# A decoder block on one core: small loads issued later, a scale block's sums cut in two, a fifth block summed on TensorE, weight loads on GpSimd's queue

## The chip, the cores and the metric

The kernel runs on one core of one Trainium2 chip (trn2). Its time is device microseconds of that core, one launch. In profiles, PE is TensorE's matmuls, PEld its weight loads, DVE is VectorE, ACT ScalarE, POOL GpSimd and SP SyncE, which only issues DMAs here.

## The reference: what is computed

One layer of a hybrid decoder block over 512 tokens of width 2048, all in float32. The part that matters here is its head:

```
mod = silu(c) @ w_ada + b_ada                     # (1, 6 * 2048); w_ada is 2048 x 12288
shift1, scale1, gate1, shift2, scale2, gate2 = split(mod, 6)
h = rms_norm(x, norm1_w) * (1 + scale1) + shift1
proj = h @ w_in                                   # 2048 x 7168: q, k, v of 8 heads, then gq, gf, gi, gg of 8 more
...
```

Behind it come the two head groups (dilated windowed attention, a gated linear recurrence), an output projection, a gated residual, and a gated MLP of width 8192 with squared ReLU. The change touches only the start, up to the second group of projections.

## The kernel before

Every product is made of three matmuls: each operand is split in a high part (float32r, made by ScalarE) and a low part (the rest, made by VectorE), and high x high, low x high and high x low are added up. A 128 x 512 matmul is the unit.

The contraction over the 2048 inputs runs over 16 blocks k of 128 rows. The gain of the norm and `1 + scale1` are both folded into the rows of `w_in`: column k of `g1c` (128 values) multiplies the weights of block k while they are split (`_split(..., scale)`, L43 and L44). So block k of the weights can't be split before column k of `g1c` exists, and that takes 2048 x 128 numbers of `w_ada` for each column. The columns come in blocks b of two (256 columns of `w_ada`, eight loads of 256 KB into `raws[b]`), one block for each pair of k. A block is summed in one of two ways:

- `summed` (blocks in `on_pe`): 16 matmuls with silu(c) as the operand, four rounds into the four row groups of a bank, then ScalarE copies, two transposes (L819), and a reduce on DVE.
- `gathered`: sixteen multiply-adds on DVE into two accumulators (L834, L836), then `to_cols`: four transposes (L159) and two row sums on ScalarE (L162).

`finish_scale` ends either (L826, L827).

`first_steps` writes out the order of PE, SP, ACT and DVE by hand (`manual_schedule`); POOL's order, and that of all engines behind it, is the scheduler's. It loads x (16 loads on SP, L845), squares it for the norm (`squares`, L785 on DVE, L788 on ACT), and takes block 0. Then it goes through the pairs k0 = 0, 2, ... 14. In pair k0, `dense(k0)` and `dense(k0 + 1)` do 18 matmuls each (six banks, three products; L883), between them lie the sums of block b = k0/2 + 1 and some transposes of x (`turn_x`, L800), and before the last third of `dense(k0 + 1)` the block is finished. At the end of the pair the weights of the next pair are split (`split_w`), which needs the columns just made. The weights of the pairs behind the first two are loaded on POOL's queue (`fetch_pair`, L767), the others and all of `w_ada` on SP.

The shift goes another way: behind the stage, background steps (`bgw`) make `shift1` from more of `w_ada` on DVE (`gemv`, L137, L139, loads L132 on SP), and then its product with some columns of `w_in`. Meanwhile `first_groups` makes the second group of projections: eight pairs again, each with two weight loads through `load_w` (L202, on SP), buffers `raw` of four. PE is given these in the scheduler's order; behind it, from the project of `gi` on, PE's order is written out.

At the very start POOL issues twelve small loads: rows of norm weights (`rows`), positions (`posi`), per-column copies of the query and key gains (`rw`, `wcol`, the latter 4 bytes a partition), two tables (`lnc_sb`, `hgm`) and the rotary frequencies (`ifq`). They are first used behind the last scale block (`mod_cols.last`), for the recurrence's bounds and the rotary tables (`rot_w`, L994 on POOL).

Of the kernel before, what the change touches and what calls it, by code (L numbers as in the profile page):

```python
# [48 lines left out]
def hybrid_block(ctx, tc, x, c, positions, norm1_w, w_ada, b_ada, w_in, q_norm_w, k_norm_w,  # L49
# [45 lines left out]
    sc_ready = dve.tensor_tensor(sc, ps_c[:, 0:NK], sc, op=ALU.mult)  # L95

    rows = ca.tile([P, P], F32, name="rows", tag="rows")
    pool.memset(rows, 0.0)
    posi = ca.tile([NT, P], I32, name="posi")
    pool.dma_start(rows[0:16], norm2_w[0].rearrange("(r p) -> r p", p=P))  # L100
    pool.dma_start(rows[16:24], attn_out_norm_w[0].rearrange("(r p) -> r p", p=P))
    pool.dma_start(rows[24:40], hg_lb_logits.rearrange("l (r p) -> (l r) p", p=P))
    pool.dma_start(rows[40:41], hg_norm_w)
    pool.dma_start(posi, positions[0].rearrange("(r p) -> r p", p=P))
    cols = const.tile([P, 48], F32, name="cols")
    n2c, aoc, hgc, posc = cols[:, 0:16], cols[:, 16:24], cols[:, 40:41], cols[:, 44:48]

    rw = ca.tile([P, 2, 32], F32, name="rw")
    wcol = ca.tile([P, 2], F32, name="wcol")
    for i, w in enumerate((q_norm_w, k_norm_w)):  # L110
        pool.dma_start(rw[:, i], w[:, 0:32].broadcast_to([P, 32]))
        pool.dma_start(wcol[:, i:i + 1], w.rearrange("o p -> p o"))
    pool.memset(wcol[0:32], 1.0)
    lnc_sb = ca.tile([P, 512], F32, name="lnc_sb")
    pool.dma_start(lnc_sb, lnc)
    hgm = ca.tile([P, NLEV, 32], F32, name="hgm")
    pool.dma_start(hgm, hgmask.rearrange("p (l t) -> p l t", t=32))
    ifq = ca.tile([P, 16], F32, name="ifq")
    pool.dma_start(ifq, inv_freq.broadcast_to([P, 16]))


    asked, marks = [None], []

# [71 lines left out]

    evacuated = []

    def load_w(view, k0, c0, n=512, eng=None, ahead=True, raws=None, behind=False, cast_behind=False, gain=None):
        with tc.high_priority() if ahead else ExitStack():
            raw = wr.tile([P, 2, n], F32, name="wraw", tag="raw", bufs=4)  # L200
            with tc.issue_after(marks[-3].ins) if behind else ExitStack():
                nc.sync.dma_start(raw, view[:, k0:k0 + 2, c0:c0 + n])  # L202
            if raws is not None:
                raws[:] = [raw[:, 0], raw[:, 1]]
            with tc.issue_after(evacuated[0].ins) if cast_behind and evacuated else ExitStack():
                return [_split(nc, wr, raw[:, j], n, eng if j else None, None if gain is None else gain[:, k0 + j:k0 + j + 1])
                        for j in range(2)]
# [38 lines left out]
    def work(name, dt=F32):  # L246
        return wk.tile([P, 512], dt, name=name, tag="wk")
# [14 lines left out]
    def first_groups(c_f, c_q, before, after):  # L262

        bt = [bank("prj", tag="mm") for _ in range(4)]
        bc = [bank("prc") for _ in range(2)]
        for k0 in range(0, NK, 2):
            before(k0)
            wt = load_w(win_v, k0, c_f, ahead=False, gain=g1c)
            wc = load_w(win_v, k0, c_q, 256, None, ahead=False, gain=g1c)
            for j in range(2):  # L270
                k = k0 + j
                ch_mm(bt, hhi[k], hlo[k], *wt[j], k == 0, k == NK - 1)
                ch_mm(bc, hhi[k], hlo[k], *wc[j], k == 0, k == NK - 1)
            after(k0)
        return bt, bc
# [439 lines left out]
    def keep(banks, name, scale=1.0):  # L715
        ts = []
        for b in banks:
            t = slot(name)
            act.activation(t, b, AF.Copy, scale=scale)
            ts.append(t)  # L720
        return ts
# [17 lines left out]
    def first_stage(c_f, c_q):  # L739

        order = mybir.EngineType
        with tc.manual_schedule(engines={order.PE, order.SP, order.Activation, order.DVE}):
            return first_steps(c_f, c_q)

    def first_steps(c_f, c_q):
# [4 lines left out]
        ssx = sm.tile([P, NT, 4], F32, name="ssx", bufs=1)  # L750
        rx = sm.tile([P, NT], F32, name="rx", bufs=1)
        raws, wraws, accs, parts = {}, {}, {}, {}
        on_pe = (0, 1, 3, 5)

        def fetch_block(b):
            raws[b] = []
# [6 lines left out]
        def fetch_pair(k0):  # L763
            wraws[k0] = []
            for c, n in ((c_f, 512), (c_q, 256)):
                raw = wr.tile([P, 2, n], F32, name="wraw", tag="raw", bufs=4)
                (pool if k0 > 2 else nc.sync).dma_start(raw, win_v[:, k0:k0 + 2, c:c + n])  # L767
                wraws[k0].append(raw)

        def split_w(k):  # L770
            parts[k] = [_split(nc, wr, raw[:, k % 2], raw.shape[2], None, g1c[:, k:k + 1]) for raw in wraws[k - k % 2]]

        def split_x(ks):
            for k in ks:
                hl = pair(k)
                hhi.append(hl[0])
                hlo.append(hl[1])
                split_to(hl, xnT[k])

        def squares(q):  # L780
            for ti in range(NT):
                jk = work("jk")
                with tc.issue_after(sc_ready.ins), tc.issue_after(sig_ready.ins):
                    if ti == NT - 1:
                        dve.tensor_tensor_reduce(jk, xs[ti][q], xs[ti][q], op0=ALU.mult, op1=ALU.add, scale=1.0, scalar=0.0,  # L785
                                                 accum_out=ssx[:, ti, q:q + 1])
                    else:
                        act.activation(jk, xs[ti][q], AF.Square, accum_out=ssx[:, ti, q:q + 1])  # L788
# [25 lines left out]
        def summed_out(b):  # L814
            t = work("acc")[:, 0:256]
            act.copy(t, accs[b][:, 0:256])
            pc = bank("pc")
            for j in range(2):
                pe.transpose(pc[:, j * P:(j + 1) * P], t[:, j * P:(j + 1) * P], ident)  # L819
            dve.tensor_reduce(g1c[:, 2 * b:2 * b + 2], pc[:, 0:256].rearrange("p (j a m) -> p j a m", j=2, m=32)[:, :, :, 0],  # L820
                              axis=AX.X, op=ALU.add)
            finish_scale(b)
# [3 lines left out]
            dve.tensor_tensor(d, d, bcol[:, NK + 2 * b:NK + 2 * b + 2], op=ALU.add)  # L826
            mod_cols.last = dve.scalar_tensor_tensor(d, d, 1.0, n1c[:, 2 * b:2 * b + 2], op0=ALU.add, op1=ALU.mult)  # L827

        def gathered(b):
            accs[b] = [work("acc")[:, 0:256] for _ in range(2)]  # L830
            for k in range(NK):
                raw, acc = raws[b][k // 2][:, k % 2], accs[b][k % 2]
                if k < 2:
                    dve.tensor_scalar(acc, raw, sc[:, k:k + 1], None, op0=ALU.mult)  # L834
                else:
                    dve.scalar_tensor_tensor(acc, raw, sc[:, k:k + 1], acc, op0=ALU.mult, op1=ALU.add)  # L836

        def gathered_out(b):
            for _ in to_cols(accs[b], g1c[:, 2 * b:2 * b + 2]):
                pass  # L840
            finish_scale(b)
# [35 lines left out]
        def dense(k, between=None):  # L877
            fine, coarse = parts.pop(k)
            first, last = k == 0, k == NK - 1
            for n, (hs, w) in enumerate(((hhi, 0), (hlo, 0), (hhi, 1))):  # L880
                for banks, ws in ((bt, fine), (bc, coarse)):
                    for j in range(len(banks)):
                        pe.matmul(banks[j], lhsT=ws[w][:, j * P:(j + 1) * P], rhs=hs[k], start=first and n == 0,  # L883
                                  stop=last and n == 2)
                if n == 1 and between:
                    between()

        def next_scale(b):
            if b in on_pe:
                summed_out(b)  # L890
            elif b < 8:
                gathered_out(b)

        for k0 in range(0, NK, 2):
            b = k0 // 2 + 1
            if k0 + 4 < NK:
                fetch_pair(k0 + 4)
            if k0 in (0, 4):
                scale_x(2 + k0 // 4, range(NT))
            if 0 < k0 < NK - 2:  # L900
                split_x((k0 + 2, k0 + 3))
            if b < 8 and b not in on_pe:
                gathered(b)
            dense(k0)
            if b in on_pe:
                summed(b, range(4))
            if k0 in (2, 6):
                turn_x(2 + k0 // 6, 0)
                turn_x(2 + k0 // 6, 1)
            dense(k0 + 1, lambda: next_scale(b))  # L910
            if k0 in (2, 6):
                turn_x(2 + k0 // 6, 2)
                turn_x(2 + k0 // 6, 3)
            if b + 2 < 8:
                fetch_block(b + 2)
            for k in (k0 + 2, k0 + 3):
                if k < NK:
                    split_w(k)
        for _ in range(16):
            bg_step()  # L920
        return bt, bc
# [9 lines left out]
    bgw.append(staggered(shift_through(4096), shift_through(3072), NK + 1, 6))  # L931
    xnT = []
    bt, bc = first_stage(4096, 3072)
    f0 = keep(bt, "f")
    hq0 = keep(bc, "gq", QS)
    with tc.issue_after(mod_cols.last.ins):
# [656 lines left out]
```

## Time and profile before

| | |
|---|---|
| median of 3 runs | 2264.39 us (2263.81 to 2265.33) |
| the profiled execution | 2263.68 us, span 2261.9 us |
| PE busy | 2215.9 us of the span |
| x landed (last piece) | 19.14 us |
| pair k0 = 0 starts on PE | 29.48 us |
| pair k0 = 14 starts on PE | 115.04 us |
| `first_groups` on PE | 123.34 to 190.14 us |
| PE's longest wait behind it | 6.17 us, up to 218.71 us |

Times in rows are microseconds from the span's start. A row of a timeline has the start, the length, the engine, the line, the operation with out<-in, the shape and a count; in square brackets stand the idle time of the engine before it and what ended it. A row of a windows view has the stretch and its length, then busy time and number of instructions of PE, PEld, DVE, ACT and POOL, the granted TensorE clock, the share of the 16 DMA engines' time that was busy, and GB/s. Matmuls are pipelined, so their ends are modelled and overlap the next start.

### The profile page before, as it was taken

To read this page: it belongs to the slowest core of one execution; us is meant where nothing else is said; L and a number is where in the kernel's file an instruction comes from. 1 tells how busy PE (TensorE), PEld (TensorE's weight loads), DVE (VectorE), ACT (ScalarE), POOL (GpSimd) and SP (SyncE) were. 2 spreads that over 40 slices of the span, in tenths; PEclk is the share of its full clock that TensorE was granted. 3 is DMA by queue.
4 is the path that set the end of the run, shared out by engine and by line. 5 is a ranking of instruction groups with operands and counts; after the bars stand their busy time and mean duration, and the time that the engine had idled before them with its cause. 6 is when DMAs were issued, how large, how long until landed. Compare 5 with 4: busy or idle time off the path is not lost.

```text
span 2261.9 us, 33188 instructions
## 1 busy us (share of the span) xinstructions
PE 2215.9 (98%) x11889; PEld 1825.1 (81%) x11889; DVE 1788.2 (79%) x2707; ACT 1093.6 (48%) x1923; POOL 449.9 (20%) x677
## 2 busy tenths in 40 slices
PE   5898999999999999999999999999999999999999
PEld 4687888888888888888887888888888888888887
DVE  4699888678886557778648988998897779967878
ACT  5356344443354464457544565565554333443332
POOL 2100022000220000003232323332232222222221
PEclk9999999999999999999999999999999999999999
DMA  9779564556555248847879789889979987998884
GB/s 327 242 257 336 177 197 163 182 180 210 184 164 187 74 142 279 275 123 261 325 276 358 288 308 390 304 301 360 337 288 368 369 315 258 348 346 312 302 298 166
DMA packets 260660, 598.30 MB, mean 265 GB/s; under 512 B 23220, under 2 KB 42432, under 8 KB 260496
## 3 DMA queue, kind: packets, MB, share of 16 engines
q1 hardware_dynamic: 183360, 327.75, 42.8%
q0 software_dynamic: 72064, 258.93, 31.2%
q10 hardware_dynamic: 5072, 9.51, 1.3%
q8 instruction: 93, 1.52, 0.3%
q14 instruction: 71, 0.58, 0.1%
HBM read 518.49 MB, written 77.61 MB: 264 GB/s over the span
## 4 chain that ended last, share of the span: by engine, by line
PE 82%; DMA 6%; DVE 5%; issue 5%; POOL 1%; ACT 1%; SPq 0%; ACTq 0%; POOLq 0%; DVEq 0%
PE f L1351 13%; PE f L1349 13%; PE f L1350 13%; PE prj L213 8%; PE prj L215 8%; PE prj L214 8%; PE f L223 3%; PE f L221 2%; PE f L222 2%; PE prj L223 1%; PE prj L222 1%; PE prj L221 1%; DMA araw<-in_w_ada_dram 1%; DMA Fl<-f_lod 1%; PE pho L643 1%
## 5 line engine op out<-in xcount | busy, mean ns | idle before, releaser
L1333 ACT CAST vhi<-raw 128x1024 fp32r<-128x1024 f32 x392 | 413.4, 1055 | 518.7 <-PE f L1351 409.5
L1334 DVE TENSOR_TENSOR vlo<-raw,vhi 128x1024 fp32r<-128x1024 f32 x392 | 474.7, 1219 | 139.4 <-ACT vhi L1333 139.1
L1350 PE MATMUL f<-vlo,Fh 128*128 128x512 f32 x1376 | 535.8, 389 | 0.5 <-DVE vlo L1334 0.4
L1351 PE MATMUL f<-vhi,Fl 128*128 128x512 f32 x1376 | 535.6, 389 | 0.4 <-DMA Fl<-f_lod 0.4
L1349 PE MATMUL f<-vhi,Fh 128*128 128x512 f32 x1376 | 536.0, 390 | 0.0
L40 ACT CAST whi<-wraw 128x512 fp32r<-128x512 f32 x304 | 187.1, 621 | 363.1 <-PE prj L215 277.8
L213 PE MATMUL prj<-whi,hi 128*128 128x512 f32 x896 | 360.4, 402 | 0.6 <-ACT aq L361 0.5
L215 PE MATMUL prj<-whi,lo 128*128 128x512 f32 x896 | 350.5, 391 | 0.2 <-DVE lo L255 0.2
L214 PE MATMUL prj<-wlo,hi 128*128 128x512 f32 x896 | 349.7, 390 | 0.0
L41 DVE TENSOR_TENSOR wlo<-wraw,whi 128x512 fp32r<-128x512 f32 x304 | 209.2, 692 | 156.4 <-ACT whi L40 151.3
L1350 PEld LDWEIGHTS f<-vlo,Fh 128*128 128x128 f32 x1376 | 258.3, 188 | 55.4 <-DVE vlo L1334 2.0
L1351 PEld LDWEIGHTS f<-vhi,Fl 128*128 128x128 f32 x1376 | 258.3, 188 | 54.6 <-DMA Fl<-f_lod 0.9
L1349 PEld LDWEIGHTS f<-vhi,Fh 128*128 128x128 f32 x1376 | 258.3, 188 | 53.4
L1317 DVE TENSOR_TENSOR raw<-raw,raw 128x1024 f32<-128x1024 f32 x224 | 269.8, 1217 | 4.3 <-DMA raw<-in_w_ff_dram 3.9
L139 DVE SCALAR_TENSOR_TENSOR acc<-araw,sc,acc 128x512 f32<-128x512 f32 x280 | 201.8, 748 | 21.0 <-DMA araw<-in_w_ada_dram 20.3
L215 PEld LDWEIGHTS prj<-whi,lo 128*128 128x128 f32 x896 | 168.6, 188 | 36.9 <-DVE lo L255 0.6
L213 PEld LDWEIGHTS prj<-whi,hi 128*128 128x128 f32 x896 | 168.8, 188 | 35.3 <-ACT ak L361 0.9
L214 PEld LDWEIGHTS prj<-wlo,hi 128*128 128x128 f32 x896 | 169.0, 189 | 32.8
L1295 POOL DMA_DIRECT2D Fh<-f_hid x112 | 79.2, 707 | 427.2 <-PE f L1351 412.1
L223 PE MATMUL f<-hi,wlo 128*128 128x512 f32 x256 | 99.9, 390 | 0.9 <-DVE wlo L41 0.9
L221 PE MATMUL f<-hi,whi 128*128 128x512 f32 x256 | 100.3, 392 | 0.0
L222 PE MATMUL f<-lo,whi 128*128 128x512 f32 x256 | 99.6, 389 | 0.0
(338 smaller groups left out, 2978.8 us busy)
## 6 DMA issues: line engine op xcount, KB each, us to landing
raw<-in_w_ff_dram SPq DMA_DIRECT2D x224, 512.0 KB, 10.3
araw<-in_w_ada_dram SPq DMA_DIRECT2D x384, 256.0 KB, 4.2
Fh<-f_hid POOLq DMA_DIRECT2D x112, 512.0 KB, 6.4
Fl<-f_lod POOLq DMA_DIRECT2D x112, 512.0 KB, 7.5
wraw<-in_w_in_dram SPq DMA_DIRECT2D x98, 512.0 KB, 4.8
Fh<-h_hid POOLq DMA_DIRECT2D x60, 512.0 KB, 6.6
Fl<-h_lod POOLq DMA_DIRECT2D x60, 512.0 KB, 7.6
f_hid<-part POOLq DMA_DIRECT2D x48, 512.0 KB, 7.4
```

The source lines that it names most:

```text
L41: _split.low = (eng or nc.vector).tensor_tensor(lo, src, hi.bitcast(F32), op=ALU.subtract)
L139: dve.scalar_tensor_tensor(acc, raw[:, k - k0], vec[:, k:k + 1], acc, op0=ALU.mult, op1=ALU.add)
L213: pe.matmul(banks[ti], lhsT=hi[:, ts], rhs=whi, start=first, stop=False)
L214: pe.matmul(banks[ti], lhsT=hi[:, ts], rhs=wlo, start=False, stop=False)
L215: pe.matmul(banks[ti], lhsT=lo[:, ts], rhs=whi, start=False, stop=last)
L223: pe.matmul(banks[j], lhsT=wlo[:, js], rhs=hi, start=False, stop=last)
L1317: dve.tensor_tensor(dst, a, b, op=ALU.subtract)
L1333: cast_done.append(act.copy(hi, src))
L1334: split_done.append(dve.tensor_tensor(lo, src, hi.bitcast(F32), op=ALU.subtract))
L1349: pe.matmul(banks[t], lhsT=fh[u][a][:, ts], rhs=whi[:, a], start=first, stop=False)
L1350: pe.matmul(banks[t], lhsT=fh[u][a][:, ts], rhs=wlo[:, a], start=False, stop=False)
L1351: pe.matmul(banks[t], lhsT=fl[u][a][:, ts], rhs=whi[:, a], start=False, stop=end)
```

## The change

- The twelve small loads and the two memsets that go with them are issued behind `fetch_pair(12)` (its second load is marked, and they wait for its issue), in place of before everything else.
- In `squares`, DVE takes two of each four pieces of x in place of one.
- `gathered` takes a range of k: the first eight k of block b + 1 stand between `split_w` of the next pair's two k, the other eight at the head of the next pair, ahead of `split_x`. Before, all sixteen stood behind `split_x`.
- Block 7 joins `on_pe`.
- `split_x` stands ahead of `scale_x`.
- In `first_groups`, the weights go on POOL's queue in place of SP's.

```diff
-    pool.memset(rows, 0.0)
-    pool.dma_start(rows[0:16], norm2_w[0].rearrange("(r p) -> r p", p=P))
...
-    pool.dma_start(ifq, inv_freq.broadcast_to([P, 16]))
...
-    def load_w(view, k0, c0, n=512, eng=None, ahead=True, raws=None, behind=False, cast_behind=False, gain=None):
+    def load_w(view, k0, c0, n=512, eng=None, ahead=True, raws=None, behind=False, cast_behind=False, gain=None, queue=nc.sync):
...
-                nc.sync.dma_start(raw, view[:, k0:k0 + 2, c0:c0 + n])
+                queue.dma_start(raw, view[:, k0:k0 + 2, c0:c0 + n])
...
-            wt = load_w(win_v, k0, c_f, ahead=False, gain=g1c)
-            wc = load_w(win_v, k0, c_q, 256, None, ahead=False, gain=g1c)
+            wt = load_w(win_v, k0, c_f, ahead=False, gain=g1c, queue=pool)
+            wc = load_w(win_v, k0, c_q, 256, None, ahead=False, gain=g1c, queue=pool)
...
-        on_pe = (0, 1, 3, 5)
+        on_pe = (0, 1, 3, 5, 7)
...
-                (pool if k0 > 2 else nc.sync).dma_start(raw, win_v[:, k0:k0 + 2, c:c + n])
+                d = (pool if k0 > 2 else nc.sync).dma_start(raw, win_v[:, k0:k0 + 2, c:c + n])
+                if k0 == NK - 4:
+                    marks[:] = [d]
...
-                    if ti == NT - 1:
+                    if ti % 2:
...
-        def gathered(b):
-            accs[b] = [work("acc")[:, 0:256] for _ in range(2)]
-            for k in range(NK):
+        def gathered(b, ks):
+            if b not in accs:
+                accs[b] = [work("acc")[:, 0:256] for _ in range(2)]
+            for k in ks:
...
+            if b < 8 and b not in on_pe:
+                gathered(b, range(8, NK))
+            if 0 < k0 < NK - 2:
+                split_x((k0 + 2, k0 + 3))
             if k0 in (0, 4):
                 scale_x(2 + k0 // 4, range(NT))
-            if 0 < k0 < NK - 2:
-                split_x((k0 + 2, k0 + 3))
-            if b < 8 and b not in on_pe:
-                gathered(b)
             dense(k0)
...
-            for k in (k0 + 2, k0 + 3):
-                if k < NK:
-                    split_w(k)
+            if k0 + 2 < NK:
+                split_w(k0 + 2)
+                if b + 1 < 8 and b + 1 not in on_pe:
+                    gathered(b + 1, range(8))
+                split_w(k0 + 3)
...
     bt, bc = first_stage(4096, 3072)
+    with tc.issue_after(marks.pop().ins):
+        pool.memset(rows, 0.0)
+        pool.dma_start(rows[0:16], norm2_w[0].rearrange("(r p) -> r p", p=P))
...
+        pool.dma_start(ifq, inv_freq.broadcast_to([P, 16]))
```

More of the change, by code (lines that the diff above doesn't have):

```diff
@@ L97, in hybrid_block @@
     rows = ca.tile([P, P], F32, name="rows", tag="rows")
-    pool.memset(rows, 0.0)
     posi = ca.tile([NT, P], I32, name="posi")
-    pool.dma_start(rows[0:16], norm2_w[0].rearrange("(r p) -> r p", p=P))
[L101 to L104, printed above, removed]
     cols = const.tile([P, 48], F32, name="cols")
@@ L109, in hybrid_block @@
     wcol = ca.tile([P, 2], F32, name="wcol")
[L110 to L113, printed above, removed]
     lnc_sb = ca.tile([P, 512], F32, name="lnc_sb")
-    pool.dma_start(lnc_sb, lnc)
     hgm = ca.tile([P, NLEV, 32], F32, name="hgm")
-    pool.dma_start(hgm, hgmask.rearrange("p (l t) -> p l t", t=32))
     ifq = ca.tile([P, 16], F32, name="ifq")
-    pool.dma_start(ifq, inv_freq.broadcast_to([P, 16]))
     asked, marks = [None], []
@@ L886, in dense @@
                     between()
[L888 to L892, printed above, removed]
         for k0 in range(0, NK, 2):
@@ L897, in first_steps @@
                 fetch_pair(k0 + 4)
+            if b < 8 and b not in on_pe:
+                gathered(b, range(8, NK))
+            if 0 < k0 < NK - 2:
+                split_x((k0 + 2, k0 + 3))
             if k0 in (0, 4):
                 scale_x(2 + k0 // 4, range(NT))
-            if 0 < k0 < NK - 2:
-                split_x((k0 + 2, k0 + 3))
-            if b < 8 and b not in on_pe:
-                gathered(b)
             dense(k0)
-            if b in on_pe:
+            if b < 8 and b in on_pe:
                 summed(b, range(4))
@@ L909, in first_steps @@
                 turn_x(2 + k0 // 6, 1)
-            dense(k0 + 1, lambda: next_scale(b))
+            dense(k0 + 1, lambda: None if b > 7 else (summed_out if b in on_pe else gathered_out)(b))
             if k0 in (2, 6):
@@ L933, in hybrid_block @@
     bt, bc = first_stage(4096, 3072)
+    with tc.issue_after(marks.pop().ins):
+        pool.memset(rows, 0.0)
+        pool.dma_start(rows[0:16], norm2_w[0].rearrange("(r p) -> r p", p=P))
+        pool.dma_start(rows[16:24], attn_out_norm_w[0].rearrange("(r p) -> r p", p=P))
+        pool.dma_start(rows[24:40], hg_lb_logits.rearrange("l (r p) -> (l r) p", p=P))
+        pool.dma_start(rows[40:41], hg_norm_w)
+        pool.dma_start(posi, positions[0].rearrange("(r p) -> r p", p=P))
+        for i, w in enumerate((q_norm_w, k_norm_w)):
+            pool.dma_start(rw[:, i], w[:, 0:32].broadcast_to([P, 32]))
+            pool.dma_start(wcol[:, i:i + 1], w.rearrange("o p -> p o"))
+        pool.memset(wcol[0:32], 1.0)
+        pool.dma_start(lnc_sb, lnc)
+        pool.dma_start(hgm, hgmask.rearrange("p (l t) -> p l t", t=32))
+        pool.dma_start(ifq, inv_freq.broadcast_to([P, 16]))
     f0 = keep(bt, "f")
```

## The prediction

> **What bounds the kernel now.** I read the page's busy shares and its chain first, then the windows by stage, then the chain and timelines of the first 220 us.
>
> ```profile
> PE 2215.9 (98%) x11889; PEld 1825.1 (81%) x11889; DVE 1788.2 (79%) x2707; ACT 1093.6 (48%) x1923; POOL 449.9 (20%) x677
> PE 82%; DMA 6%; DVE 5%; issue 5%; POOL 1%; ACT 1%; SPq 0%; ACTq 0%; POOLq 0%; DVEq 0%
> 0.00:20.00 20.00, 0.45 (x1) 0.18 (x1) 3.39 (x13) 9.59 (x27) 9.00 (x24) 1.00 0.88 283
> 20.00:120.00 100.00, 89.42 (x492) 65.76 (x493) 63.42 (x159) 45.79 (x94) 9.78 (x13) 0.98 0.85 271
> 120.00:200.00 80.00, 80.00 (x360) 66.17 (x359) 75.62 (x148) 47.97 (x98) 4.41 (x9) 1.00 0.88 301
> 200.00:220.00 20.00, 13.83 (x63) 11.30 (x62) 20.00 (x35) 11.88 (x25) 0.15 (x1) 0.90 1.03 376
> 220.00:2262.00 2042.00, 2032.16 (x10978) 1681.73 (x10976) 1625.75 (x2355) 978.34 (x1681) 426.58 (x631) 1.00 0.74 261
> ```
>
> The window rows give the busy time of PE, PEld, DVE, ACT and POOL, then clock, DMA share and GB/s. PE idles 46.0 us of the 2261.9 us span: 19.6 before 20 us, 10.6 between 20 and 120, none between 120 and 200, 6.2 between 200 and 220, and 9.8 in the 2042 us behind. Everything the change touches lies before 220 us. Behind that PE never stops for long, so a lead that PE has at 220 us should reach the end whole; the question is what lead it gets.
>
> **Part 1: the start.** The first 19 us load x.
>
> ```profile
> 13.64 5.50 DMA xs<-in_x_dram
> 4.00:12.00 8.00, 0.45 (x1) 0.18 (x1) 1.21 (x6) 3.24 (x11) 4.04 (x11) 1.00 0.90 256
> 12.00:18.00 6.00, 0.00 (x0) 0.00 (x0) 1.40 (x4) 3.55 (x11) 1.93 (x4) 1.00 1.05 385
> lnc_sb<-in_lnc_dram POOLq DMA_DIRECT2D x1, 256.0 KB, 7.7
> hgm<-in_hgmask_dram POOLq DMA_DIRECT2D x1, 96.0 KB, 7.7
> L785 DVE CUSTOM_DVE_ANT_0 jk<-xs x4: 682/692/693, 8.7 to 19.3; 128x512 f32<-128x512 f32 x4
> L788 ACT ACTIVATE jk<-xs x12: 617/626/630, 8.5 to 18.6; 128x512 f32<-128x512 f32 x12
> ```
>
> The chain goes from the last piece of x (issued 13.64, landed 19.14) to its square and on. From 4 to 12 us, with the small loads on POOL's queue, the DMA engines moved 256 GB/s at a share of 0.90; from 12 to 18 it was 385. The change takes the small loads out of there. Full rate over those 8 us would be 1.03 MB or 2.7 us more, and the two tables (lnc, hgm: 0.36 MB) leave another 0.9 us of room: 3.6 us at most. Part of the slow rate may be the queue's own start, so I take 3.0. The lower bound is the bytes alone, 0.9. Negative I exclude: nothing is added before x. The scale blocks and weights follow x on the same queue, so they and PE's start move with it.
>
> Squares: ACT had 12 and DVE 4, now 8 each. The last piece is squared by DVE before and after (0.69 us). ACT's twelve, at 0.62 from 8.5 us, could have ended at 16, so this edit is worth nothing at an x that lands at 16.1, and keeps ACT from being the bound if x lands sooner. DVE's four more (2.8 us) lie in its waits for x. I count 0.
>
> **Part 2: the pairs of k (20 to 123 us).** Each pair costs PE 36 matmuls; the scale columns for the next pair must exist before PE can start it.
>
> ```profile
> 41.17 1.19 PE L883 MATMUL prj<-hi,whi 128*128 128x512 f32 x4
> 50.38 0.85 PE L159 MATMUL pc<-ident,acc 128*128 128x128 f32 x4 [1.21 <-DVE acc L836]
> 54.84 1.20 PE L883 MATMUL prj<-hi,whi 128*128 128x512 f32 x4 [1.34 <-ACT whi L43]
> 65.70 1.19 PE L883 MATMUL prj<-hi,whi 128*128 128x512 f32 x4
> 79.36 1.20 PE L883 MATMUL prj<-hi,whi 128*128 128x512 f32 x4 [1.35 <-ACT whi L43]
> 90.23 1.19 PE L883 MATMUL prj<-hi,whi 128*128 128x512 f32 x4
> 92.33 1.29 DVE L255 TENSOR_TENSOR lo<-xnT,hi 128x512 fp32r<-128x512 f32 x2
> 94.06 5.62 DVE L836 SCALAR_TENSOR_TENSOR acc<-araw,sc,acc 128x256 f32<-128x256 f32 x14
> 99.44 0.92 PE L159 MATMUL pc<-ident,acc 128*128 128x128 f32 x4 [2.11 <-DVE acc L836]
> 100.05 2.02 PE L883 MATMUL prj<-hi,wlo 128*128 128x512 f32 x4
> 101.47 0.16 DVE L826 TENSOR_TENSOR g1c<-g1c,bcol 128x2 f32<-128x2 f32 x1 [1.78 <-ACT pc L162]
> 102.72 1.50 PE L883 MATMUL prj<-hi,whi 128*128 128x512 f32 x4
> 111.85 0.30 PE L159 MATMUL pc<-ident,acc 128*128 128x128 f32 x1 [1.71 <-DVE acc L836]
> 115.04 1.20 PE L883 MATMUL prj<-hi,whi 128*128 128x512 f32 x4 [0.41 <-ACT whi L43]
> 100.00:110.00 10.00, 10.00 (x39) 7.71 (x37) 7.71 (x19) 4.12 (x10) 0.00 (x0) 0.83 0.49 140
> ```
>
> The starts of pairs 2, 4, 6, 8, 10, 12 and 14 are 41.17, 54.84, 65.70, 79.36, 90.23, 102.72 and 115.04. Pairs 4 and 8, whose block (3, 5) is summed on TensorE, take 10.86 and 10.87. Pairs 2, 6, 10 and 12, whose block (2, 4, 6, 7) DVE sums, take 13.67, 13.66, 12.49 and 12.32, and in each PE waits for DVE's last acc. In DVE's order the two lows of x (lo, 1.29) stand ahead of all sixteen accs.
>
> - Halves round the low part: the sixteen accs stay the same work, but lo moves behind them, into the 1.78 us in which DVE waits for ACT's row sums anyway. DVE's last acc comes 1.29 sooner. Pairs 2 and 6 can use what PE waits there, 1.2 each; their second wait (1.34, on ACT behind the copies of xnT) moves along but stays. Pair 10 gains 1.3. The price: the second k's low weights come half the accs later (3.1 us), 5.3 us behind the pair's start, and PE reads them as the last third of the second k, 6.8 us or more behind it. Cover 1.5; if it went, the gain of 1.3 would go with it. So the bounds are 0 and 1.3 a pair.
> - The wait of 2.11 in pair 10 is followed by matmuls at half speed (2.02 for four that take 1.07 to 1.2 elsewhere; granted clock 0.83 in that window). Most of it is hidden behind ACT; 1.50 against 1.20 in the next pair's first four is what shows: 0.3.
> - Fifth block on TensorE: pair 12 becomes a pair like 4 and 8: 12.32 to 10.87, 1.45. DVE loses 6 us of accs there and idles, since its order is written out. ScalarE copies one row more, as in pairs 4 and 8.
> - ACT's scale_x and split_x change places: both are done inside the same pair. Nothing.
>
> Sum of part 2: 1.2 + 1.2 + 1.3 + 0.3 + 1.45 = 5.4 (bounds 1.4 to 5.6: block 7 alone, or all of it).
>
> The Trainium skill ("TensorE: Matmul & The Clock Gate", Part 1) has the clock halve after an idle window of about 3.4 us. Here 2.11 was enough, and 1.71 in pair 12 was not; by that page alone pair 10 would owe its 0.3 to something else, and the sum would be 5.1.
>
> **Part 3: the small loads in their new place.** They are issued behind pair 12's weights (81.46 to 82.90).
>
> ```profile
> 92.32 1.45 POOL L767 DMA_DIRECT2D wraw<-in_w_in_dram  x2 [9.42 <-DVE wlo L44]
> 80.00:92.00 12.00, 11.93 (x77) 8.65 (x76) 5.03 (x13) 4.68 (x10) 1.44 (x2) 1.00 0.73 225
> ```
>
> POOL stands idle 9.42 us there and the DMA engines run at 0.73. Twelve issues at not over 0.73 (the row's two weight loads took 1.45) and two memsets, one of them behind a landing (7.7 for the tables above), are 8.8 + 7.7: they may push pair 14's loads back some 7 us. Those are first read for pair 14 (115.04): cover 15 us or more, cost 0. The small tiles are first used behind the last block's columns, near 114: cover 20 us, cost 0.
>
> **Part 4: weights on POOL's queue (123 to 190 us).**
>
> ```profile
> 123.34 0.39 PE L221 MATMUL prc<-hi,whi 128*128 128x512 f32 x1
> 190.14 0.39 PE L213 MATMUL prj<-whi,hi 128*128 128x512 f32 x1
> wraw<-in_w_in_dram SPq DMA_DIRECT2D x20, 512.0 KB, 6.1
> wraw<-in_w_in_dram POOLq DMA_DIRECT2D x6, 512.0 KB, 5.2
> 121.65 3.34 SPq L202 DMA_DIRECT2D wraw<-in_w_in_dram  x2
> 133.86 7.41 SPq L202 DMA_DIRECT2D wraw<-in_w_in_dram  x3
> 142.50 1.56 POOL L994 TENSOR_TENSOR rot_w<-sinT,rw 128x64 f32<-128x64 f32 x4 [48.73 <-DVE sinT L988]
> 169.78 0.49 DVE L137 TENSOR_SCALAR acc<-araw,sc 128x512 f32<-128x512 f32 x1 [1.00 <-DMA araw<-in_w_ada_dram]
> 218.71 1.11 PE L159 MATMUL pc<-ident,acc 128*128 128x128 f32 x4 [6.17 <-DVE acc L153]
> ```
>
> Sixteen weight loads leave SP, where they wait for a free buffer (7.41 us for three) with the scale tiles queued behind them. On POOL they cost 0.73 of issue each (above) and nothing is queued behind them but rot_w and each other; they land no later there (5.2 against 6.1). PE does not wait in this stretch, so the loads themselves bring it nothing. What can gain is DVE, which is full from 120 on and ends late: PE stands 6.17 at 212 to 218.7 for it. Scale tiles that come sooner take away DVE's one wait for them, 1.00. I take 1.0; bounds 0 and, if DVE's order fell so that its backlog vanished, 6.2. The eight pairs of this stage take PE from 123.34 to 190.14, 8.35 each; with two pairs of buffers a load may come some 8 us late before PE sees it.
>
> The Trainium skill ("DMA: Bandwidth & Descriptors", Issuing engines are not separate DMA queues) says that all issuing queues share the same DMA engines and a second one saves only issue time. By that page part 4 is worth 0 and the sum is 8.4; the 7.41 us that SP stood is more than issue time.
>
> **Sum.** 3.0 + 5.4 + 1.0 = 9.4 us. The profiled execution took 2263.68, of which 1.8 lies outside its span; 2263.7 - 9.4 = 2254.3. It was 0.7 faster than the median of the runs (2264.39), so I predict 2255.0.
>
> **Rivals.**
>
> - x lands hardly sooner, since the slow rate up to 12 us is the queue's start: 0.9 instead of 3.0, 2257.1. For it: 0.90 share, the engines were not idle. Against: the rate recovers just as POOL's loads end.
> - The lead is lost at 212 us: DVE (20.00 of 20.00) or the scale tiles behind it (DMA share 1.03) end when they did, and PE only waits longer at the same transposition, 6.2 + 8.4. Then 2264, no change. For it: both are full there. Against: DVE's part of that work starts right behind the last pair's low weights, which come sooner too, and its accs of block 7 are gone.
> - The backlog vanishes: 5.2 us more than forecast, 2249.8.
> - Slower: rot_w stands in POOL's stream ahead of a weight load. If the third pair's loads (121.65) had to stand behind rot_w (142.50 to 146.5), they would be 25 us late; landing (5.2) and split would have it ready at 153, PE takes that pair at 123.34 + 16.7 = 140.0, so PE loses 13 less the 9.4 gained: 2268.0. From about 22 us late (9 of cover here, 9.4 of gain, 4 of margin) it decides the sign. For it: rot_w waits long on DVE. Against: another place in the stream avoids it.
>
> **How the numbers follow.** Forecast 0.62; x hardly sooner 0.13; lead lost 0.12; backlog gone 0.07; POOL blocked 0.06. A run cannot tell less than 0.2% (4.5 us) from no change. Faster: the first two and the fourth, 0.82, less 0.02 for sums of small misses; same 0.13; slower 0.07. Range 2248 to 2260: the bounds of the parts add up to 2.3 and 15.4 us of gain, of which it takes in 4 to 16, and it leaves out the lost lead and the blocked queue, 0.18.
>
> **What the next profile would show.** Part 1: the window 4 to 12 us above 320 GB/s, x landed near 16. Part 2: pairs 2, 6 and 10 shorter by 1.2 to 1.6, pair 12 near 10.9, no half clock near 95. Part 4: no wait on scale tiles near 160, PE's wait before its late transposition not over 6.2. Wrong if that wait has grown by the lead, if POOL stands before weights, or if DVE, which asks for a block's first tiles some 2 us sooner, then waits for them.

## The result, and the profile after

After: 2260.31 us, median of 20 runs (2257.27 to 2266.36); before, 20 runs on the same chip: 2264.78 (2262.44 to 2266.01, and one of 5783.21). The ratio is 0.9982, interval 0.9975 to 0.9989: 4.1 us gained (4.5 between the medians). The forecast was 2255.0, a gain of 9.4, in a range of 2248 to 2260. The profiled execution of after took 2260.87 us.

The windows of after (columns as before), with the page's busy line ahead of them:

```profile
PE 2218.3 (98%) x11919; PEld 1825.0 (81%) x11919; DVE 1784.7 (79%) x2700; ACT 1090.2 (48%) x1912; POOL 461.0 (20%) x693
```

```profile
4.00:12.00 8.00, 0.45 (x1) 0.18 (x1) 3.11 (x12) 3.14 (x10) 0.00 (x0) 1.00 0.98 325
12.00:18.00 6.00, 0.58 (x4) 0.22 (x4) 3.14 (x10) 2.38 (x8) 0.01 (x1) 1.00 1.04 345
...
20.00:120.00 100.00, 94.58 (x545) 70.82 (x542) 63.76 (x160) 48.71 (x99) 19.74 (x32) 1.00 0.88 285
120.00:200.00 80.00, 79.62 (x357) 65.22 (x356) 74.75 (x140) 47.78 (x102) 11.81 (x19) 1.00 0.89 309
200.00:220.00 20.00, 13.45 (x54) 10.80 (x53) 19.15 (x33) 13.30 (x26) 0.00 (x0) 0.83 0.89 327
220.00:2259.00 2039.00, 2027.64 (x10953) 1677.19 (x10951) 1619.76 (x2345) 972.50 (x1667) 426.21 (x631) 1.00 0.74 261
```

Between 4 and 12 us the DMA engines moved 325 GB/s where they moved 256. Behind 220 us PE idles 11.4 us (2039.00 less 2027.64) where it idled 9.8. The last piece of x, from the chain, and PE's timeline of the pairs and of every wait that matters behind them:

```profile
10.78 5.75 DMA xs<-in_x_dram
```

```profile
38.19 1.20 PE L871 MATMUL prj<-hi,whi 128*128 128x512 f32 x4
50.66 1.20 PE L871 MATMUL prj<-hi,whi 128*128 128x512 f32 x4 [1.34 <-ACT whi L43]
61.52 1.20 PE L871 MATMUL prj<-hi,whi 128*128 128x512 f32 x4
73.97 1.20 PE L871 MATMUL prj<-hi,whi 128*128 128x512 f32 x4 [1.34 <-ACT whi L43]
84.84 1.19 PE L871 MATMUL prj<-hi,whi 128*128 128x512 f32 x4
92.84 0.85 PE L144 MATMUL pc<-ident,acc 128*128 128x128 f32 x4 [0.91 <-DVE acc L824]
95.97 1.19 PE L871 MATMUL prj<-hi,whi 128*128 128x512 f32 x4 [0.89 <-ACT whi L43]
106.96 1.20 PE L871 MATMUL prj<-hi,whi 128*128 128x512 f32 x4
115.25 0.39 PE L206 MATMUL prc<-hi,whi 128*128 128x512 f32 x1
175.74 1.21 PE L208 MATMUL prj<-hi,wlo 128*128 128x512 f32 x4 [0.38 <-DVE wlo L44]
211.93 1.11 PE L144 MATMUL pc<-ident,acc 128*128 128x128 f32 x4 [6.55 <-DVE acc L138]
1019.90 0.50 PE L208 MATMUL f<-hi,wlo 128*128 128x512 f32 x1 [1.24 <-DVE wlo L41]
1222.84 0.50 PE L1348 MATMUL f<-vlo,hi 128*128 128x512 f32 x1 [0.45 <-DVE vlo L1332]
1228.12 0.44 PE L1377 MATMUL pt<-ident,s 128*128 128x128 f32 x2 [2.01 <-DVE s L1396]
1710.80 0.50 PE L1349 MATMUL f<-vhi,Fl 128*128 128x512 f32 x1 [0.76 <-DMA Fl<-f_lod]
```

x landed at 16.53 (19.14 before). The rows at L871 are the starts of pairs 2, 4, 6, 8, 10, 12 and 14. So pairs 2, 6, 10 and 12 took 12.47, 12.45, 11.13 and 10.99, each 1.2 to 1.4 less than before, and the first group starts at 115.25, 8.09 us sooner. The forecast had 8.4 for parts 1 and 2. Then PE gives the lead back: matched against the same matmuls of before, it leads by 8.1 at 124 us, 7.1 at 225, 6.3 at 1030, 3.1 at 1240 and 2.8 at the end (places by the times of before; at 225 the half clock behind the wait near 212 is over in both). Where PE stood 6.55, 1.24, 2.01 and 0.76 from 211.93 on, it had stood 6.17, 0.64, 1.56 and 0.43 before.

### The profile page after: what moved, and what is told of

Same layout as the page of the kernel before. It is cut to its first block, busy times and chain, and to the rows that moved or that the text cites. A ratio compares the mean times of both kernels' runs of the same rounds, so it can differ in the third digit from the quotient of the medians.

```text
span 2259.1 us, 33229 instructions
## 1 busy us (share of the span) xinstructions
PE 2218.3 (98%) x11919; PEld 1825.0 (81%) x11919; DVE 1784.7 (79%) x2700; ACT 1090.2 (48%) x1912; POOL 461.0 (20%) x693
## 4 chain that ended last, share of the span: by engine, by line
PE 71%; issue 9%; DMA 9%; DVE 7%; POOL 3%; ACT 1%; SPq 0%; POOLq 0%; ACTq 0%; DVEq 0%
PE f L1349 10%; PE f L1348 10%; PE f L1347 10%; PE prj L198 8%; PE prj L200 7%; PE prj L199 7%; PE f L208 2%; PE f L207 2%; PE f L206 2%; DMA Fl<-h_lod 2%; PE prj L871 1%; DMA f_lod<-fs 1%; PE prj L206 1%; PE prj L208 1%; PE prj L207 1%
## 6 DMA issues: line engine op xcount, KB each, us to landing
raw<-in_w_ff_dram SPq DMA_DIRECT2D x224, 512.0 KB, 10.6
```

## The experiments

The late loss was the question. Each version was run against the kernel before on its own chip; ratios are to that.

| version | us (runs) | ratio to before, interval |
|---|---|---|
| start only | 2261.82 (11) | 0.9986, 0.9977 to 0.9995 |
| POOL's queue only | 2265.25 (11) | 1.0003, 0.9994 to 1.0012 |
| pairs only | 2264.21 (11) | 0.9995, 0.9987 to 1.0004 |
| after, weights back on SP | 2260.63 (11) | 0.9985, 0.9976 to 0.9994 |
| after, small loads at the start | 2263.24 (11) | 0.9993, 0.9985 to 1.0002 |
| after + 8 sums in pair 12 | 2255.66 (5) | 0.9961, 0.9949 to 0.9974 |
| after + 48 small matmuls | 2255.87 (5) | 0.9961, 0.9947 to 0.9974 |
| after + 96 | 2260.59 (11) | 0.9982, 0.9973 to 0.9991 |
| after + 128 | 2263.64 (11) | 0.9989, 0.9980 to 0.9998 |
| before + 16 | 2266.81 (11) | 1.0008, 0.9999 to 1.0017 |
| before + 32 | 2270.50 (11) | 1.0021, 1.0012 to 1.0030 |
| 8 sums in pair 12 + 48 | 2252.75 (5) | 0.9944, 0.9931 to 0.9956 |
| 8 sums in pair 12 + 96 | 2255.01 (5) | 0.9956, 0.9943 to 0.9968 |
| 6 sums in pair 12 + 48 | 2253.45 (5) | 0.9945, 0.9932 to 0.9957 |

**The parts alone, and second profiles of both kernels.** The start alone has the small loads behind pair 12's weights and the new squares; POOL's queue alone has `queue=pool` in `first_groups`.

> The changed kernel once more, for a second profile. In the first one PE leads the kernel before by 8.1 us at pair 14, 7.2 near 990 us and 2.8 at the end; behind 225 us the instruction streams of both kernels are the same. Theory A (the late loss is chance: how the loads of two queues interleave while the DMA engines are full, and where a wait of PE falls in the clock's window): the lead up to 900 us comes out within 0.3 of the first profile, and what is lost behind 990 us differs by over 1 us or falls on other waits. Theory B (a kernel that leads runs into the same full DMA queue, so the lead is cut at fixed places): the same waits, within 0.5 us each (1.24 near 1020, 0.45 near 1223, 2.0 near 1228 and 0.76 near 1711), and half clock at 1229 again.

> The kernel before once more, for a second profile. Theory A: its late waits (0.64 near 1026, 1.56 near 1233, 0.43 near 1714) change too, by up to 1 us, and a wait above 1.7 may bring half clock. Theory B: they stay within 0.2 us.

> The kernel before with the small loads moved behind pair 12's weights and the squares two and two, nothing else. The prediction has 3.0 us for it. Expected: the first pair of k starts at 26.5 in place of 29.5. If a lead reaches the end whole, 2261.8 (3.0 under the kernel before). If the late stage eats leads (theory B), 1 us under it or less.

> The kernel before with only the sixteen weight loads of the second group on GpSimd's queue. The prediction has a gain of 1.0 for it, the rival 0. The trace of the changed kernel rather shows a lead that falls by 0.9 between 130 and 190 us: by that, 0 to 1 us slower than the kernel before, with the wait near 212 us longer than 6.2.

The start is worth 3.2 us, as forecast (3.0), and its lead stays: 3.7 at 225 us, 4.1 at 1240, 3.8 at the end. POOL's queue is worth nothing. A chance lead of 0.5 up to pair 12 was -0.2 at 124 us, ahead of the loads that were moved: half clock had followed the wait of 2.10 in pair 12. From 124 to 219 it fell to -1.04. DVE waited 1.68 for the scale tiles near 170 (1.00 before), and PE 6.52 for DVE (6.17):

```profile
111.24 0.30 PE L159 MATMUL pc<-ident,acc 128*128 128x128 f32 x1 [2.10 <-DVE acc L836]
```

```profile
170.64 0.49 DVE L137 TENSOR_SCALAR acc<-araw,sc 128x512 f32<-128x512 f32 x1 [1.68 <-DMA araw<-in_w_ada_dram]
```

```profile
219.75 1.12 PE L159 MATMUL pc<-ident,acc 128*128 128x128 f32 x4 [6.52 <-DVE acc L153]
```

The second profile of after had the same 2.01 near 1226, and that execution took 2257.4. So the wait belongs to the kernel; the stretch of half clock that followed it in the first profile (a window of it is below) does not. The second profile of before (2265.88) had its late waits within 0.8 us of the first one's, with one more of 1.24 at 1714.

**Pairs only, and after with one part taken back.**

> The kernel before with the pairs' edits alone: halves round the low part, the order of the splits, block 7 on TensorE. Small loads stay at the start, squares as before, weights on SP. Prediction's theory (the lead that the pairs give reaches the end whole): pair 0 near 29.5, pairs 2, 6, 10 and 12 at 12.5, 12.5, 11.1 and 11.0, PE's first group behind the pairs 5.1 to 5.4 us sooner than before, and the time 5.1 to 5.4 us below before, near 2259.7. Rival (the pairs' lead is largely lost behind 123 us: -3.2 for the start and +0.7 for POOL's queue leave only -1.6 of the -4.1 for the pairs): the same pairs and the same lead at 123, but 1 to 2.5 us below before, with PE's waits near 175, 212, 1019 and 1228 together 3 us longer than in before.

```diff
-        on_pe = (0, 1, 3, 5)
+        on_pe = (0, 1, 3, 5, 7)
...
+            if b < 8 and b not in on_pe:
+                gathered(b, range(8, NK))
```

> The kernel after with the sixteen weight loads of the first groups back on SP's queue. Prediction's theory (POOL's queue is worth 1.0): 1 us slower than after, 2261.3. Rival (POOL's queue loses the lead it should keep, as it did alone: 1.6 us between 115 and 219): 0.7 to 1.5 us faster than after, 2259 to 2259.6; no PE wait near 175, and PE's lead over before at 219 us 0.8 to 1.6 above after's 7.2. If neither: the same as after, and the losses lie elsewhere.

> The kernel after with the small loads back at the start. If the parts add up: the start's 3.0 go, 2263.2 to 2263.5, pair 0 near 29.5. If late places take back a part of any lead: less than that is lost, 1 to 2 us (2261.5 to 2262.5), with PE's waits near 1019 and 1228 smaller than after's 0.9 to 1.2 and 2.0.

Pairs only: PE's lead grew from 0.7 at pair 0 to 5.8 at 124 us, 5.1 from the pairs, and was 1.9 at the end. The rival held: of the 5.4 that the pairs were to bring, 1.1 us came out (0.0005 of 2264), and the interval allows for no gain at all. The wait at 212, 7.23 long, took 1.2 of the lead, the stretch near 1230 with its wait of 2.00 took 1.5. With the small loads back at the start, after loses 2.9 between the medians: that part adds up. Taking POOL's queue back changed nothing that can be told (0.9985 against 0.9982), with the wait near 212 longer by as much as PE came sooner:

```profile
211.82 1.12 PE L144 MATMUL pc<-ident,acc 128*128 128x128 f32 x4 [7.64 <-DVE acc L138]
```

**The wait near 212.** Since block 7 went to TensorE, DVE stands 6.06 us in pair 12 of after:

```profile
105.42 0.17 DVE L807 TENSOR_REDUCE g1c<-pc 128x2 f32<-128x8 f32 x1 [6.06 <-PE pc L806]
```

Eight of the sixteen background steps (`gemv`'s sums) were moved there:

```diff
+            if k0 == NK - 4:
+                for _ in range(8):
+                    bg_step()
...
-        for _ in range(16):
+        for _ in range(8):
```

> The kernel after, with eight of the sixteen background sums (0.74 each) that DVE does at the first group moved into pair 12, where DVE stands idle some 6 us since block 7 went to TensorE. If the wait near 212 is DVE's amount of work and a lead at 220 reaches the end: PE's wait falls from 6.5 to 1 to 2, the lead over before at 220 rises from 7.2 to about 12, and the time falls by 3 to 5 to 2255.5 to 2257.5. If a kernel with a lead loses it to the full DMA queues further on (waits near 1019, 1228, 1711): the wait at 212 is gone all the same, but those three grow by as much, and the time stays 2259 to 2260. If the scale tiles' landings set that wait (DMA share 1.03 there): it stays near 6.5.

The wait at 212 is gone, and a smaller one stands at 184:

```profile
184.03 0.80 PE L198 MATMUL prj<-whi,hi 128*128 128x512 f32 x1 [2.67 <-ACT f L704]
```

The lead at 225 us was 12.9, and 3.1 of it went behind that (after: 4.3 of 7.1, in its second profile 1.7 of 8.0; weights on SP: 2.0 of 7.0; pairs only: 2.7 of 4.6; loads first: 1.6 of 3.7; start only: none of 3.8). The loss does not grow with the lead, so that theory falls. Near 1230 every one of these versions with block 7 on TensorE loses 0.6 to 3.3 us, and none without it does.

**What block 7 moves.** PE's own instructions come by DMA, on queue 8. The list of queues, before and after:

```profile
q8 instruction: 93, 1.52, 0.3%
```

```profile
q8 instruction: 94, 1.54, 0.3%
```

Each is one packet of 16 KB, and takes one of the 16 DMA engines about 1 us. One comes every 28.4 us where PE is full, and in that time PE does some 125 matmuls and 125 weight loads (133 and 132 in the 30 us below): one load is 256 instructions or nearly so. Block 7 on TensorE adds 32 sums and spares two transposes: 30 matmuls (11919 against 11889) with their weight loads, 60 instructions, nearly a quarter of a load. So all later loads should come 6 to 7 us forward, by that estimate. Near 1195 to 1225 the DMA engines are full:

```profile
1195.00:1225.00 30.00, 29.92 (x133) 24.44 (x132) 23.22 (x23) 13.44 (x15) 7.08 (x10) 1.00 1.03 383
```

There a piece of weights (`raw`) lands late or not, DVE starts on it at once and works in a fixed order, and 11 us later PE stands for DVE's `s`. In before, POOL issues the Fh load at 1204.07 (POOL's timeline), one instruction load falls between 1217.8 and 1219.8 (the queues in that window), and the piece lands for DVE at 1221.71 (DVE's timeline), 17.6 behind POOL's issue; PE waits 1.56:

```profile
1204.07 0.71 POOL L1295 DMA_DIRECT2D Fh<-h_hid  x1 [4.41 <-PE f L1351]
```

```profile
q8 instruction: 1, 0.02, 3.4%
```

```profile
1221.71 1.23 DVE L1317 TENSOR_TENSOR raw<-raw,raw 128x1024 f32<-128x1024 f32 x1 [1.72 <-DMA raw<-in_w_ff_dram]
```

```profile
1232.87 0.44 PE L1379 MATMUL pt<-ident,s 128*128 128x128 f32 x2 [1.56 <-DVE s L1398]
```

In after the issue is at 1197.72, the instruction load between 1205 and 1207, while all the pieces are still on their way, and the piece lands at 1216.96, 19.2 behind the issue:

```profile
1197.72 0.70 POOL L1293 DMA_DIRECT2D Fh<-h_hid  x1 [3.23 <-PE f L1349]
```

```profile
q8 instruction: 1, 0.02, 3.5%
```

```profile
1216.96 1.22 DVE L1315 TENSOR_TENSOR raw<-raw,raw 128x1024 f32<-128x1024 f32 x1 [2.16 <-DMA raw<-in_w_ff_dram]
```

To test it, the loads were moved and nothing else: small matmuls that nothing reads, on the same line of the code, in PE's idle time at the start.

```diff
-    sc_ready = dve.tensor_tensor(sc, ps_c[:, 0:NK], sc, op=ALU.mult)
+    sc_ready = dve.tensor_tensor(sc, ps_c[:, 0:NK], sc, op=ALU.mult); [pe.matmul(ps_c[0:32, P:P + 8], lhsT=ident[:, 0:32], rhs=crow[:, 0:8], start=True, stop=True) for _ in range(96)]
```

> The kernel after with 96 small matmuls (32x8) in PE's idle time at the start (7.9 to 17.4 us); nothing reads them. PE's instructions are loaded 16 KB at a time through one of the DMA engines, about 1 us each and one every 28.4 us; block 7's 32 more transpositions brought that load 7 us forward, in all six runs with the pairs' edit into the full DMA stretch near 1195 to 1225. 96 matmuls with their weight loads are 192 instructions, three quarters of a load: the loads return to where the kernel before has them. Theory (where PE's instruction load falls sets the loss there): counted from the Fh issue at 1197.7, the load at +14.3 in place of +7.9, the weights issued at +2.2 land at 17.0 to 17.6 in place of 18.7 to 19.2, PE's wait at the transpositions near 1228 falls from 2.0 to 0.8 to 1.5, the one near 1711 from 0.8 to 0.4, and the time is 1 to 2.5 us below after's (2258 to 2259.3). Rival (the lead itself runs into the full queues, whatever PE loads): load and landing part, the wait stays 2.0, the time 2260.3.

> The control: the kernel after with 128 such matmuls at the start, 256 instructions, one whole load, so that the later loads fall where after has them. Theory: load at +7.9, landing at 18.7 to 19.2, PE's wait 2.0 and the time as after (2260 to 2261). If the small matmuls help or harm by themselves (a warm clock, a later start), it shows here as in the version with 96.

> The kernel before with 32 such matmuls at the start, 64 instructions, as many as block 7 on TensorE adds, and nothing else. Theory: PE's instruction load moves from +14.3 to +7.9 after the Fh issue near 1204.1, the weights issued at +2.2 land at 18.2 to 19.3 in place of 16.8 to 17.6, PE's wait near 1231 grows from 0.8 to 1.6 toward 2.0 (it is capped there by DVE's own order), the one near 1712 from 0.4 to 0.8, and the time is 0.5 to 1.5 us above before. Rival: no change in landing or time.

> Eight background sums in pair 12 (2255.7 alone) and the 96 small matmuls together. Theory: the two gains add up, 2253.5 to 2255; PE's lead over before keeps 11 of the 12.9 us that it has at 223. Rival: 2255.7, with the wait of 2.0 near 1217 still there.

The count was wrong: PE's timeline shows each small matmul twice.

```profile
7.56 10.36 PE L95 MATMUL ps_c<-crow,ident 128*32 128x8 f32 x191 [0.94 <-DVE sc L95]
```

So 32 and 96 moved the loads by half a load, not by a quarter and three quarters, into the full stretch again (4.3 us ahead of POOL's issue in after + 96, 1.6 behind it in before + 32), and the landings stayed late, or became so: 18.7 and 19.2. Before + 32 took 5.8 us more than before. In its profile 2.9 of that go near 1029, at a wait of 1.95 with half clock behind it (granted clock 0.57 in the window), and 1.4 near 1239, at a wait of 2.01; that the first of these too is due to a load is not shown.

```profile
1029.16 0.50 PE L223 MATMUL f<-hi,wlo 128*128 128x512 f32 x1 [1.95 <-DVE wlo L41]
```

```profile
1029.00:1033.00 4.00, 3.84 (x10) 3.02 (x11) 4.00 (x8) 4.00 (x8) 2.01 (x4) 0.57 0.80 257
```

The control with 128 (two whole loads) had loads, landing and wait as in after, and queue 8 brought two packets more than in after, which fits 256 instructions to a load; its small matmuls end near 21.5 and start pair 0 4.0 us later, enough for the 3.3 us between the medians. The next set had the counts that were wanted:

> The kernel after with 48 of the small matmuls at the start. In the versions with 32 and 96 each of them showed as two matmuls with two weight loads, so that 32 moved PE's instruction loads by half a load, 96 by one and a half, and 128 by two. 48 are 192 instructions, three quarters of a load: what was wanted. Theory (where PE's instruction load falls): counted from the Fh issue near 1197.7, loads at -13 to -14.5 and +14 to +15 and none between; the weights issued at +2.2 land at 16.8 to 17.6, PE's wait near 1228 is 0.8 to 1.6, and the time 1 to 2.5 us below after's, 2258 to 2259.5. Rival: loads there, but landing and wait as in after, 2260.4.

> The kernel before with 16 of the small matmuls at the start, 64 instructions, as many as block 7 on TensorE adds. Theory: loads at about -21 and +7.5 after the Fh issue near 1204; landing of the weights issued at +2.2 at 18.2 to 19.3 in place of 16.8 to 17.6, PE's wait near 1231 1.8 to 2.0, and the time 0.7 to 2 us above before's. Rival: 2264.5 as before, with its wait.

> Eight background sums in pair 12 and 48 of the small matmuls: 2255.7 without them. Theory: PE's instruction load leaves the full stretch, 2253.5 to 2255, landing at 16.8 to 17.6 after the Fh issue and a wait below 1.7 near 1217. Rival: 2255.0 to 2255.7, wait 2.0.

> Six background sums in pair 12 in place of eight, with 48 of the small matmuls. With eight, PE waits 2.7 near 184 for DVE's low weights and not at all at 212; with none, 6.5 at 212. If DVE's work up to 212 is one sum that is only shared out between these two waits: the wait at 184 falls to about 1, one of 1 to 2 us comes back at 212, and the time is within 1 us of the version with eight. If the wait at 184 is DVE's order there (eight is too many at that place): 1 to 2 us faster.

After + 48: loads at -10.9 and +14.9; POOL's issue at 1197.98, the piece lands at 1214.17, and PE waits 0.59:

```profile
1197.98 0.71 POOL L1293 DMA_DIRECT2D Fh<-h_hid  x1 [3.25 <-PE f L1349]
```

```profile
1214.17 1.23 DVE L1315 TENSOR_TENSOR raw<-raw,raw 128x1024 f32<-128x1024 f32 x1 [0.61 <-DMA raw<-in_w_ff_dram]
```

```profile
211.47 1.12 PE L144 MATMUL pc<-ident,acc 128*128 128x128 f32 x4 [6.55 <-DVE acc L138]
...
1225.79 0.44 PE L1377 MATMUL pt<-ident,s 128*128 128x128 f32 x2 [0.59 <-DVE s L1396]
```

Its wait at 212 is that of after, 6.55, and its lead over before is 6.7 at 225 us, 7.0 at 1240 and 6.7 at the end. It takes 2255.87, 4.4 us less than after, by work that nothing reads. The 4.4 lies between a median of 20 runs and one of five, and the two intervals just part (0.9975 and 0.9974). Before + 16 is the reverse: the load moves to +7.5, the landing from 17.6 to 19.3, PE's waits to 1.89 (1028) and 2.00:

```profile
1225.52 1.23 DVE L1317 TENSOR_TENSOR raw<-raw,raw 128x1024 f32<-128x1024 f32 x1 [2.00 <-DMA raw<-in_w_ff_dram]
```

```profile
1236.68 0.44 PE L1379 MATMUL pt<-ident,s 128*128 128x128 f32 x2 [2.00 <-DVE s L1398]
```

Its 2266.81 is 1.9 above before; the interval just reaches 1. Six sums in pair 12 spoke against the theory, and were profiled a second time, as was after + 48:

> A second look at the version with 48 small matmuls. If the place of PE's instruction loads sets the landing: loads at -11 and +15 again, the weights issued at +2.2 land at 16 to 17.6, PE's wait near 1226 is below 1.6. If the first look was chance: landing 18 to 19 and a wait of 2.0.

> A second look at the one profile that spoke against it: loads at -10.5 and +14.9, and yet landing at 18.6 and a wait of 2.0. If that was chance (two queues' packets fall in another order): landing 16 to 17.6 this time. If this kernel has another reason: 18.6 again.

The two executions took 2257.25 and 2254.96. So the second profile of after + 48 is only 0.15 faster than that of after: it was 1.1 us behind it at 225 us, by a later start, and gained 2.1 in the stretch near 1228, where neither had half clock.

All profiles of the stretch, counted from POOL's Fh issue (instruction loads of 16 KB from 15 us ahead of it to 25 behind; landing of the piece issued 2.2 us behind it, 3.1 in before + 32; PE's wait for `s`):

| | loads | landing | PE's wait |
|---|---|---|---|
| before, two profiles; start only; POOL only | -14.7 to -13.9 and +14.2 to +14.4 | 16.8 to 17.6 | 0.79 to 1.56 |
| after + 48, two profiles; 8 sums + 48 | -11.0 to -10.3 and +14.8 to +14.9 | 16.0 to 16.5 | 0.59 |
| 6 sums + 48, two profiles | -10.9, -10.6 and +14.8 | 17.8, 18.6 | 1.74, 2.00 |
| after + 96; 8 sums + 96 | -4.7, -4.3 and over +24 | 17.8, 18.7 | 1.75, 2.01 |
| before + 32 | +1.6 | 19.2 | 2.01 |
| before + 16; after, two profiles; after + 128; weights on SP; loads first; pairs only; 8 sums | +7.5 to +8.0 | 18.2 to 19.5 | 2.00 to 2.01 |

With no load between -10 and +14 the piece lands by 17.6 in seven of nine profiles; with one there, in none of eleven. The gap is narrow: the earliest of the late ones is 17.8. The first piece of the group, issued some 0.5 us behind POOL's load, shows the same: 8.8 to 9.1 in the first two rows, 9.3 to 10.3 in all others. That is later by about the 1.1 us that a load takes; how one packet on one DMA engine delays a piece was not followed. The exception is one kernel, late in both profiles from the first piece on, with its loads where after + 48 and 8 sums + 48 have theirs. Why it is late stays open, so the place of the load explains 18 of 20 profiles and not all. The 8 KB loads of the other engines (queue 14) are not the cause: after and after + 48 both have them at -0.5 to +0.1 and +9.2.

**The version that beats both.** Eight sums in pair 12 with 48 small matmuls: 2252.75 us, ratio 0.9944 (0.9931 to 0.9956), 12.7 us below before. Near 212 PE does not stand any more; near 184 it stands 2.06 and near 1220 0.59:

```profile
200.00:220.00 20.00, 20.00 (x92) 16.55 (x91) 18.38 (x33) 11.47 (x24) 0.00 (x0) 1.00 0.56 190
```

Six sums (2253.45) are not to be told from eight. That DVE's work up to 212 is one sum, shared out between the two places, is not shown: with six PE stands 1.84 and 1.10 near 184, in its two profiles, and no wait came back at 212, where 1 to 2 us were expected.

## Why the prediction was wrong, by its own steps

- Part 1, start: 3.0 forecast, 2.99 at pair 0 (29.48 to 26.49; 3.9 in the second profile, so this start varies), 3.2 alone. The window rose above 320 GB/s and x landed near 16, as foretold. Right.
- Part 2, pairs: 5.4 forecast, 8.09 less 2.99, or 5.1, in after and 5.1 alone. Pairs 2 and 6 kept their wait of 1.34 and the half clock near 95 went, as foretold. Pair 12 took 10.99 (near 10.9 foretold). Right as a price of PE's time in the pairs. The 0.3 for half clock was partly luck: in POOL's queue only and in before + 16, whose pairs are those of before, it came behind the wait in pair 12 (2.10, 2.12) and not behind the one in pair 10 (2.09, 2.10). The step for block 7 left something out: it costed 32 more matmuls by their time, and not by the instructions that they put into PE's stream.
- Part 3, small loads in their new place: 0. The start alone kept its lead to the end. Right.
- Part 4, weights on POOL's queue: 1.0 forecast, nothing measured, alone (1.0003) and in company (0.9982 against 0.9985). The step that failed is "Scale tiles that come sooner take away DVE's one wait for them, 1.00": that wait grew, to 1.68 alone and, with DVE asking sooner, to 2.15 in after. The text had named this as a way to be wrong. The Trainium skill ("DMA: Bandwidth & Descriptors", Issuing engines are not separate DMA queues) would have had it at 0, and the runs agree.

```profile
162.81 0.49 DVE L122 TENSOR_SCALAR acc<-araw,sc 128x512 f32<-128x512 f32 x1 [2.15 <-DMA araw<-in_w_ada_dram]
```

- The sentence that failed is the one in the first part: "so a lead that PE has at 220 us should reach the end whole". In after 4.3 of 7.1 us went behind 225. The start alone showed that a lead can reach the end, and after + 48 that this one could: with PE's instruction loads elsewhere all of its 6.7 arrived, and its median, 2255.87, stands 0.9 from the forecast. So most of the miss, by the medians 4.4 of 5.3 us, goes with the place of the 16 KB loads, which moving them alone shows. Part 4's 1.0 would fill the 0.9 that is left, but medians of five runs do not tell that much.
- How it comes about: in the profiled execution of after, 0.45 and 2.01 of waiting near 1222 to 1228, against 0.59 with the loads away, and half clock behind it (0.57 granted in the window below; 3.41 us long, so 1.7 lost), which the second profile of after did not have. Matched against after + 48, the stretch costs 4.2 us with the half clock, and 2.1 between the two second profiles, without it. How often half clock comes in the runs that were not profiled is not known, so the 4.4 between the medians can't be split between the two.

```profile
1229.00:1233.00 4.00, 4.00 (x19) 3.62 (x18) 1.99 (x3) 3.63 (x6) 0.00 (x0) 0.57 0.94 309
```

- The rival of a lead lost at 212 took a little: the wait should not pass 6.2 and was 6.55 in after, 7.23 in pairs only, and of the 8.1 at 124 us 1.0 was gone at 225. Most of the lead passed there, as the text argued against that rival.

The loads near 1019 and 1711 were not settled: PE's waits there differ between versions (0.30 to 1.95, 0.31 to 1.26) without one order by the place of the load.

## What to carry to other kernels

A lead is worth what the tightest stretch behind it lets through: before adding up gains at the start, look for the stretches where the DMA engines are full and an engine's wait ends on a landing. Any edit that adds or takes away instructions on TensorE moves all its later instruction loads; where a stretch is full, try the same kernel with a few idle instructions at a place that costs nothing, before judging the edit itself. And look for the engine that an edit leaves idle: here the 6 us of DVE in pair 12 were worth as much as the whole change.

## What the runs showed of the hardware that was not expected

- TensorE's instructions are loaded while it runs, 16 KB (256 instructions) in one packet of 0.9 to 2.3 us on one DMA engine, 93 times in the kernel before. The Trainium skill ("Trainium Architecture — The Big Picture", The software stack) tells of the instruction streams being brought in when the kernel is loaded; the queue rows here show them during the run. The Trainium skill ("DMA: Bandwidth & Descriptors", Queues, rings and completion order) has each DMA engine take turns between its queues packet by packet, which fits one packet of 16 KB holding up weights in packets of 2 KB; the packets' turns themselves were not looked at.
- Twelve loads with pieces as small as 4 bytes a partition cost far more than their bytes: from 4 to 12 us all queues together moved 256 GB/s with them and 325 without. The queue of x moved 1.61 MB in those 8 us, and 2.55 MB in after.
- Half clock after waits shorter than the prediction knew: 1.24 us at 1714 in the second profile of before, 2 us behind one of 0.44, and after the wait of 1.74 to 2.01 near 1228 in seven of thirteen profiles, never after one of 0.59 to 1.56 there (seven profiles). Each lasted 3.41 us. The Trainium skill ("TensorE: Matmul & The Clock Gate", Part 1) tells of a free-running window of that length; the length agrees, and these waits were shorter than one window.
